# Hybrid attention and state-space trunk: the second layer's state-space preparation placed behind the first FFN's second tile, and the kernel slices stored group by group

## The chip, the cores and the metric

One core of a Trainium2 chip runs the whole program. The metric is device time in microseconds of one execution; the runs shown give a median of three.

## The reference, cut to what matters

Two layers work on 528 positions (16 learned ones and 512 inputs) of width 1024, in float32. Each layer projects the normed residual, feeds part of the result to four attention heads and part (512 channels, 32 groups of 16) to a diagonal state-space mixer, joins both with an output projection, and adds a gated FFN of width 2816.

```python
for l in range(DEPTH):
    z = _rms_norm(h, norm_mix_g[l]) @ w_in[l]
    c_q, c_kv, k_r, u = jnp.split(z, splits, axis=-1)
    attn = _mla_mixer(c_q, c_kv, k_r, ...)
    ssm = _ssm_mixer(u, ssm_a_re[l], ssm_a_im[l], ssm_log_dt[l], ...)
    mixed = jnp.concatenate([_rms_norm(attn, attn_out_g[l]), _rms_norm(ssm, ssm_out_g[l])], axis=-1)
    h = h + mixed @ w_o[l]
    hn = _rms_norm(h, norm_ffn_g[l])
    h = h + (jax.nn.silu(hn @ w_gate[l]) * (hn @ w_up[l])) @ w_down[l]
return _rms_norm(h, final_norm_g)[:, M:]
```

Inside the mixer a group's 64 complex states follow `x[t] = lam * x[t-1] + B u[t]`, and `y = Re(C x) + d * u`. `lam`, `B` and `C` come from the parameters alone, so everything made of them can be prepared before the activations are there.

## The kernel before, in words

Activations lie transposed: channels on the 128 partitions, positions along the row. Residual tiles are `h[0]` to `h[7]`. A linear layer loads weights into one of three raw buffers (`wload`, from L245), casts them on ScalarE to a rounded part `whi`, subtracts on VectorE or GpSimd to get the rest `wlo`, and multiplies both with the split activations (`product`, from L257): three terms per block of 128 x 128. In layer 0 the projections in `FULL` use plain float32 weights instead. The output products are w_oa on the attention result (`am`) and w_os on the state-space result (`sm`); their evaluation on VectorE scales the sum into `wo`, adds it to `h`, splits the new `h` into `x` for the FFN and adds its squares.

The FFN works in three phases of 7, 7 and 8 hidden tiles (`FFN_PHASES`). A tile is a gate product `ga` and an up product `ua` of 48 matmuls each; `ev_up` evaluates them on VectorE and ScalarE into `hid`. A phase ends with the products `da` back to width 1024.

The state-space part runs in chunks of 8 positions. `prep_small` (from L389) makes powers of `lam` in about 180 narrow VectorE operations, 32 groups wide; `prep_tables` (from L566) makes tables `tab` on GpSimd; `prep_mats` (from L597) makes, for each of 8 units of 4 groups, the input matrix `Xt`, the output matrix `C` and the kernel slices `K` of the 8 taps, which TensorE computes (`pk`, L643) and which go to DRAM. The last tap also holds the skip `d`. A slice of one input row is a window of the row of taps, shifted by one tap per position, with zeros behind: a transfer (L658) reads the overlapping windows from 16 partitions and writes the block of 128 x 512 that `ssm_out` (from L746) later loads as `mt` and uses as matmul weights `mt3`. Each `ya` sums a product with `mt3` on the inputs (L756) and one with `C` on the states (L757).

`prep` is a generator. Layer 0 runs it woven with its own input projection; layer 1's is advanced by `step(nxt, 2, NXT[0])` in layer 0's FFN, two pieces after every hidden tile from `NXT[1]` on, and finished by `run(nxt)`. The tile framework then sets the order of the instructions on each engine itself, from a timeline that it simulates and a priority that follows the program text; an instruction that waits for nothing can so be placed well ahead of where the text has it. Weight loads and these transfers are issued by SP, in one queue; loads of the preparation's parameters by ScalarE.

```python
            if i >= NXT[1]:
                step(nxt, 2, NXT[0])
```

The helper `after(ins)` (L203) gives a context in which the framework places instructions only behind `ins`; `latest(e)` (L199) is the instruction that engine e was given last.

Of the kernel before, what the change touches and what calls it, by code (L numbers as in the profile page):

```python
# [26 lines left out]
HC = 16  # L27
CT = 8
# [28 lines left out]
PTR = (0,0,1,0,1)  # L57
SCB = (0,1,0,0)
GLU_IN = (9,5)
NXT = (0, 0)  # L60
MB = (2,4,2,3,2)
SPL = 1
NRV = 0
# [38 lines left out]
def trunk(ctx: ExitStack, tc: tile.TileContext, A, out, dbg=None):  # L102
    nc = tc.nc
# [10 lines left out]
    V, S, P, T = nc.vector, nc.scalar, nc.gpsimd, nc.tensor  # L114
# [21 lines left out]
    def prep_tile(tag, w, bufs, name=None, dt=F32):  # L136
        return scope["prep"][1].tile([128, w], dt, tag=tag, name=name or tag, bufs=bufs)
# [61 lines left out]
    def latest(e):  # L199

        return next(i for i in reversed(nc.cur_bb.bb.instructions) if i.engine == e.engine)

    def after(ins):  # L203
        return tc.issue_after(ins) if ins is not None else nullcontext()

    def mul(e, o, a, b):
        tt(e, o, a, b, ALU.mult)
# [15 lines left out]
    h = [cp.tile([128, L], F32, name=f"h{k}") for k in range(8)]  # L223
# [160 lines left out]
    prm, mats = {}, {}  # L384
# [212 lines left out]
    def prep_mats(l, u, ea, eb):  # L597

        g0 = u * 4
        gs = slice(g0, g0 + 4)  # L600
        raw = prep_tile("bc", 448, BUFS[0])
        nc.scalar.dma_start(raw[:, 0:256], A["ssmbc"][l, u])
        b1, b2, c1, c2 = (raw[:, i * 64:(i + 1) * 64].rearrange("p (g h) -> p g h", g=4) for i in range(4))

        def bh(ap):
            return ap[:, gs].unsqueeze(2).to_broadcast([128, 4, HC])

        bb1, bb2, t = (raw[:, i * 64:(i + 1) * 64].rearrange("p (g h) -> p g h", g=4) for i in (4, 5, 6))
        for o, x, y, ci in ((bb1, b1, b2, "CIn"), (bb2, b2, b1, "CIp")):
            mul(ea, o, x, bh(prm["CR"]))  # L610
            mul(ea, t, y, bh(prm[ci]))
            tt(ea, o, o, t, ALU.add)
        yield

        def power(E, dst, tmp, x1, x2, p1, p2, n):
            def bt(ap):
                return ap.unsqueeze(2).to_broadcast([128, 4, n, HC])

            def bp(ap):
                return ap[:, :, gs].rearrange("p t g -> p g t").unsqueeze(3).to_broadcast([128, 4, n, HC])  # L620

            mul(E, dst, bt(x1), bp(p1))
            mul(E, tmp, bt(x2), bp(p2))
            tt(E, dst, dst, tmp, ALU.add)

        v4 = lambda ap: ap.rearrange("p (g t h) -> p g t h", g=4, h=HC)
        X, tmp = (prep_tile("XC", 576, BUFS[1], n)[:, 0:512] for n in ("X", "Xt"))
        power(ea if ea is eb else on('X', u), v4(X), v4(tmp), bb1, bb2, prm["prr"][:, 1:9], prm["pir"][:, 1:9], 8)
        pt = ps1.tile([128, 512], F32, tag="one", name="pt")
        for g in range(4):  # L630
            T.transpose(pt[:, g * 128:(g + 1) * 128], X[:, g * 128:(g + 1) * 128], ident)
        XT = tmp
        S.copy(XT, pt)
        nc.sync.dma_start(mats[l, u][:, 0:512], XT)
        yield
        C, tmp = (prep_tile("XC", 576, BUFS[1], n) for n in ("C", "Ct"))
        power(eb if ea is eb else on('C', u), v4(C), v4(tmp), c1, c2, prm["prs"], prm["pim"], 9)
        dst = mats["k", l, u] = dp.tile([128, 1024], F32, name=f"k{l}_{u}")
        nc.sync.dma_start(dst[:, 512:1024].rearrange("p (g w) -> p g w", g=4),
                          C.rearrange("p (g w) -> p g w", g=4)[:, :, 0:128])  # L640
        pk = ps1.tile([128, 512], F32, tag="one", name="pk")
        for g in range(4):
            T.matmul(pk[0:16, g * 128:(g + 1) * 128], bb1[:, g, :], C[:, g * 144 + 16:g * 144 + 144], start=True, stop=True)  # L643

        if u < KB:
            prm["K", u] = prep_tile(f"K{u}", 1024, 1)[0:16]
            P.memset(prm["K", u][:, 512:1024], 0.0)
        K = prm["K", u % KB]
        S.copy(K[:, 0:512].rearrange("p (t h g) -> p g t h", g=4, h=HC), pk[0:16].rearrange("p (g t h) -> p g t h", g=4, h=HC))
        skip = prep_tile("skip", 64, 2)[0:16].rearrange("p (g h) -> p g h", h=HC)  # L650
        last = K[:, 448:512].rearrange("p (h g) -> p g h", h=HC)
        mul(P, skip, ident[0:16, 0:HC].unsqueeze(1).to_broadcast([16, 4, HC]),
            skips[:, l * G + g0:l * G + g0 + 4].unsqueeze(2).to_broadcast([16, 4, HC]))
        tt(P, last, last, skip, ALU.add)
        yield
        windows = [list(d) for d in K[:, 0:512].unsqueeze(1).ap]
        windows[1] = [64, CT]
        nc.sync.dma_start(dst[:, 0:512].rearrange("(j h) w -> h j w", h=HC), bass.AP(K.tensor, K.offset, windows))  # L658
        yield

    def prep(l, ea, eb):
# [84 lines left out]
    def ssm_out(l, u, U, sv, yd):  # L746
        q, hf = divmod(u, 2)
        s = 2 if l == DEPTH - 1 else 0
        n = NC - s
        mt = ssm_tile("mt", 1024, MB[2])  # L750
        mt3, c8 = mt[:, 0:512].rearrange("p (m g) -> p g m", g=4), mt[:, 512:1024]
        nc.sync.dma_start(mt, mats["k", l, u])
        ya = ps1.tile([128, 512], F32, tag="one", name="ya")
        for i in range(4):
            o, c = slice(i * n, (i + 1) * n), slice(i * NC + s, (i + 1) * NC)
            T.matmul(ya[:, o], mt3[:, i, :], U[:, c], start=True, stop=False)  # L756
            T.matmul(ya[:, o], c8[:, i * 128:(i + 1) * 128], sv[:, c], start=False, stop=True)  # L757
        ys = ssm_tile("ys", HALF, 1)
        S.copy(ys[:, 0:4 * n], ya[:, 0:4 * n])
        nc.sync.dma_start(yd[q].rearrange("j (h g) c -> (j h) g c", h=HC)[:, hf * 4:hf * 4 + 4, :],  # L760
                          ys[:, 0:4 * n].rearrange("p (g c) -> p g c", c=n))
        yield
# [75 lines left out]
    def layer(l, nin, nout, nxt):  # L838
# [81 lines left out]
        def step(g, n=1, later=LATER[l]):  # L920
            for _ in range(n):
                tc.cur_priority += later
                next(g, None)
                tc.cur_priority -= later
# [320 lines left out]
        for ph in FFN_PHASES:  # L1245
            hid = []
            last = t0 + ph == NHT
            for i in range(t0, t0 + ph):
                wg = wload(A["w_gate"][l, i], V if i >= ONP[0] else P)
                ga = acc2("ga")  # L1250
                product(ga, wg, 0, nf.xs, nat, {PINF[1]: nf.spread} if i == 1 else {})
                if i == 0:
                    nf.F()
                wu = wload(A["w_up"][l, i], V if i >= ONP[1] else P)
                ua = acc2("ua")
                product(ua, wu, 0, nf.xs, nat, {PINF[0]: nf.summed} if i == 0 else {})
                nf.R()
                ev_up(i, ga, ua, hid)
                if i >= NXT[1]:
                    step(nxt, 2, NXT[0])  # L1260
            def down(m):
                return wload(A["w_down"][l, m][:, t0 * 128:(t0 + ph) * 128])

            def add(m, acc, c):
                hv = halves(h[m][:, c[0]:c[1]])
                tt(V, hv, pv(acc, c[1] - c[0]), hv, ALU.add)

            ends = last and l == DEPTH - 1
            for m in range(6 if ends else 8):
                w = down(m)  # L1270
                acc = acc2("da")
                product(acc, w, 0, hid, nat)
                add(m, acc, nat)
                if last:
                    nout.add(m)
                if ends and m in SCALED:
                    S.activation(h[m][:, own], h[m][:, own], AF.Copy, scale=fgain(m))
            if ends:

                ws, parts = [down(m) for m in (6, 7)], []  # L1280
                for c in ((NM, HALF + 8), (HALF + 8, L)):
                    for m in (6, 7):
                        acc = acc2("da")
                        product(acc, ws[m - 6], 0, hid, c, {TAIL[0]: parts[0].pin} if parts and m == 7 else {})
                        add(m, acc, c)
                        nout.sq.add(h[m], cols=c)
                    with after(parts[0].spread if parts and NR1 else None):
                        parts.append(Final(c, nout, "one" if parts else "norm"))
                parts[0].out(OUT[0], parts[1].then)
                parts[1].out(OUT[1])  # L1290
            t0 += ph
# [17 lines left out]
    for k in range(8):  # L1309
        if k in SQP:  # L1310
            t = single("sq")
# [110 lines left out]
```

## Time and profile before

| | |
|---|---|
| median of 3 runs | 1368.3 us (1367.06 to 1368.87) |
| profiled execution | 1364.46 us |
| its span, first to last instruction | 1362.7 us |
| mean granted TensorE clock | 0.972 |
| busy: TensorE, weight loads, VectorE | 1290.8, 1167.3, 817.0 us |
| busy: ScalarE, GpSimd | 442.0, 374.2 us |
| DMA | 145.94 MB, mean 107 GB/s |

Layer 0's input projection and attention take the first 240 us, its output products lie around 240 to 350 us, its FFN runs to about 736 us; layer 1 follows to the end. Matmul ends are modelled, so a busy share near 100% says that no wait was seen, not that the engine ran at its peak. The granted clock is the share of the full 2.4 GHz that the throttle allowed.

### The profile page before, as it was taken

The numbers are of one execution on the slowest core, as the hardware profiler recorded it, in microseconds if no ns is written. First come the engines' busy times: TensorE is split into PE (matmuls) and PEld (weight loads), VectorE is DVE, ScalarE is ACT, GpSimd is POOL, SyncE is SP. The second block draws the span as 40 slices with busy tenths as digits, with TensorE's granted clock in tenths as the row PEclk, the third lists the DMA queues.
The fourth block names the chain that finished last, engine by engine and source line by source line (L and its number), as shares of the span: only waits on it lengthen the run. The fifth ranks groups of instructions, "written<-read, shape, count | busy, mean of one in ns | idle before, by whom it ended". The sixth has DMA issues, their size and how long they took to land.

```text
span 1362.7 us, 20603 instructions
## 1 busy us (share of the span) xinstructions
PE 1290.8 (95%) x8242; PEld 1167.3 (86%) x8242; DVE 817.0 (60%) x1539; ACT 442.0 (32%) x725; POOL 374.2 (27%) x365
## 2 busy tenths in 40 slices
PE   9889999857999999999999999998999999999996
PEld 7677888847999999999999999888878888788885
DVE  8866574999654357447664468873854345435545
ACT  4212453323232123223233235661432223222231
POOL 3634233476611005205312354347200000000001
PEclk9899999978899999999999999999999999999998
DMA  5566543212433323434343535312133332232331
GB/s 190 168 169 158 149 125 90 72 47 67 133 108 101 106 90 111 105 99 120 105 109 109 186 100 177 107 47 71 54 95 95 91 105 92 82 106 93 93 94 62
DMA packets 76816, 145.94 MB, mean 107 GB/s; under 512 B 22704, under 2 KB 42672, under 8 KB 76720
## 3 DMA queue, kind: packets, MB, share of 16 engines
q1 hardware_dynamic: 73120, 141.32, 35.4%
q10 hardware_dynamic: 3600, 3.30, 0.8%
q8 instruction: 65, 1.06, 0.3%
q14 instruction: 31, 0.25, 0.1%
HBM read 121.17 MB, written 23.43 MB: 106 GB/s over the span
## 4 chain that ended last, share of the span: by engine, by line
PE 80%; DVE 11%; DMA 1%; ACT 1%; issue 1%; POOL 0%; DVEq 0%; ACTq 0%; SPq 0%; POOLq 0%
PE da L277 18%; PE ua L277 18%; PE ga L277 18%; PE acc L277 9%; PE acc L265 3%; PE ya L756 2%; PE pvo L1099 1%; PE ya L757 1%; DVE h L197 1%; PE va L721 1%; PE sc L1039 1%; DVE wo L197 1%; DVE sq L197 1%; DVE x L311 1%; PE pvo L1102 1%; PE nrb L371 1%
## 5 line engine op out<-in xcount | busy, mean ns | idle before, releaser
L253 ACT CAST whi<-raw 128x1024 fp32r<-128x1024 f32 (+3 forms) x174 | 174.2, 1001 | 567.1 <-issue 191.0
L277 PE MATMUL ga<-x,whi 128*128 128x264 f32 (+1 forms) x1056 | 227.3, 323 | 6.8 <-ACT x L310 4.8
L277 PE MATMUL ua<-x,whi 128*128 128x264 f32 (+1 forms) x1056 | 225.6, 322 | 0.0
L277 PE MATMUL da<-hid,whi 128*128 128x264 f32 (+2 forms) x1088 | 224.8, 315 | 0.0
L277 PEld LDWEIGHTS ga<-x,whi 128*128 128x128 f32 x1056 | 164.5, 190 | 24.6 <-ACT x L310 5.0
L277 PEld LDWEIGHTS da<-hid,whi 128*128 128x128 f32 x1088 | 167.1, 188 | 14.1 <-ACT whi L253 0.4
L277 PEld LDWEIGHTS ua<-x,whi 128*128 128x128 f32 x1056 | 164.9, 190 | 15.8
L197 DVE TENSOR_TENSOR wlo<-raw,whi 128x1024 fp32r<-128x1024 f32 (+1 forms) x130 | 166.7, 1282 | 13.1 <-ACT whi L253 10.7
L277 PE MATMUL da<-hid,wlo 128*128 128x264 f32 (+2 forms) x544 | 143.6, 317 | 0.2
L277 PE MATMUL ga<-x,wlo 128*128 128x264 f32 (+1 forms) x528 | 142.5, 324 | 0.7 <-POOL wlo L197 0.7
L277 PE MATMUL ua<-x,wlo 128*128 128x264 f32 (+1 forms) x528 | 142.3, 324 | 0.0
L197 POOL TENSOR_TENSOR wlo<-raw,whi 128x1024 fp32r<-128x1024 f32 (+2 forms) x44 | 95.0, 2160 | 134.3 <-ACT whi L253 115.8
L197 DVE TENSOR_TENSOR h<-da,h 128x528 f32<-128x528 f32 (+2 forms) x50 | 33.9, 677 | 133.1 <-PE da L277 132.9
L197 POOL TENSOR_TENSOR o<-h,nr 128x256 f32<-128x256 f32 x8 | 6.1, 798 | 364.8 <-ACT nr L375 364.8
L197 DVE TENSOR_TENSOR g<-ua,R 128x528 f32<-128x528 f32 (+1 forms) x44 | 30.8, 700 | 122.1 <-PE ua L277 122.0
L277 PEld LDWEIGHTS da<-hid,wlo 128*128 128x128 f32 x544 | 90.1, 188 | 8.3 <-DVE wlo L197 1.1
L277 PEld LDWEIGHTS ga<-x,wlo 128*128 128x128 f32 x528 | 88.4, 190 | 8.7 <-POOL wlo L197 1.1
L277 PEld LDWEIGHTS ua<-x,wlo 128*128 128x128 f32 x528 | 88.4, 190 | 7.4
L197 DVE TENSOR_TENSOR g<-ga,nr 128x528 f32<-128x528 f32 (+1 forms) x44 | 30.8, 699 | 90.6 <-PE ga L277 88.5
L265 PE MATMUL acc<-x,raw 128*128 128x264 f32 x320 | 78.3, 403 | 0.1
L265 PEld LDWEIGHTS acc<-x,raw 128*128 128x128 f32 x320 | 62.7, 199 | 11.7 <-ACT x L683 0.5
L277 PE MATMUL acc<-sm,whi 128*128 128x264 f32 (+1 forms) x256 | 47.2, 310 | 18.1 <-DVE wo L197 16.6
(291 smaller groups left out, 2243.7 us busy)
## 6 DMA issues: line engine op xcount, KB each, us to landing
raw<-w_gate SPq DMA_DIRECT2D x44, 512.0 KB, 3.6
raw<-w_up SPq DMA_DIRECT2D x44, 512.0 KB, 3.6
raw<-w_down SPq DMA_DIRECT2D x32, 448.0 KB, 3.4
raw<-w_in SPq DMA_DIRECT2D x20, 512.0 KB, 3.8
mat<-mat SPq DMA_DIRECT2D x16, 528.0 KB, 4.0
mt<-k SPq DMA_DIRECT2D x16, 512.0 KB, 4.6
raw<-w_down SPq DMA_DIRECT2D x16, 512.0 KB, 3.6
mat<-tab SPq DMA_DIRECT2D x16, 272.0 KB, 2.9
```

Of the source, the lines that this page charges most:

```text
L197: e.tensor_tensor(out=o, in0=a, in1=b, op=op)
L253: S.copy(hi[:, :n], raw[:, :n])
L265: T.matmul(acc[:, a, 0:hw], w[0][:, off + k * 128:off + (k + 1) * 128], xs[k][:, c0 + a * hw:c0 + (a + 1) * hw], start=k == 0, stop=k == n ...
L277: T.matmul(acc[:, a, 0:hw], wt[:, c], xs[k][:, xi, c0 + a * hw:c0 + (a + 1) * hw], start=j == 0, stop=j == len(terms) - 1)
L311: V.scalar_tensor_tensor(out=lo, in0=src, scalar=scale, in1=hi.bitcast(F32), op0=ALU.mult, op1=ALU.subtract)
L371: T.matmul(p[:, a - c0:b - c0], y[0:b - a, j:j + 1].to_broadcast([b - a, 128]), ident[0:b - a, 0:b - a], start=True, stop=True)
L721: T.matmul(va[:, i * NC:(i + 1) * NC], xt[:, i * 128:(i + 1) * 128], U[:, i * NC:(i + 1) * NC], start=True, stop=True)
L756: T.matmul(ya[:, o], mt3[:, i, :], U[:, c], start=True, stop=False)
L757: T.matmul(ya[:, o], c8[:, i * 128:(i + 1) * 128], sv[:, c], start=False, stop=True)
L1039: T.matmul(o, qn[hd][:, qs], kn[hd][:, ks], start=True, stop=False)
L1099: T.matmul(acc[:, a, 0:w], vs[hd // 2, j][0:sn, hd % 2 * 128:hd % 2 * 128 + 128], PT[j][0:sn, 0, c:c + w].bitcast(F32), start=j == 0, stop ...
L1102: T.matmul(acc[:, a, 0:w], vs[hd // 2, j][0:sn, vi, hd % 2 * 128:hd % 2 * 128 + 128], PT[j][0:sn, pi, c:c + w], start=j == 0 and z == 0, s ...
```

## The change

`NXT[1]` becomes 1: the preparation of layer 1 starts after hidden tile 1 instead of tile 0, and its first two pieces are placed only behind the last ScalarE instruction given out by then (the cast of tile 1's `hid`). It has two pieces fewer among the tiles, and so two more in `run(nxt)`. The row of taps gets one block of 256 per group, 128 taps and 128 zeros, instead of the four groups side by side within a tap; `mt3` then reads 128 neighbouring numbers per group instead of every fourth. The windows of one group are contiguous, and a store goes out as four transfers, one per group, each with runs of 512 bytes instead of 2 KB.

```diff
-NXT = (0, 0)
+NXT = (0, 1)
...
-            P.memset(prm["K", u][:, 512:1024], 0.0)
+            P.memset(prm["K", u].rearrange("p (g w) -> p g w", g=4)[:, :, 128:256], 0.0)
...
-        S.copy(K[:, 0:512].rearrange("p (t h g) -> p g t h", g=4, h=HC), pk[0:16].rearrange("p (g t h) -> p g t h", g=4, h=HC))
+        K4 = K.rearrange("p (g w) -> p g w", g=4)
+        S.copy(K4[:, :, 0:128], pk[0:16].rearrange("p (g w) -> p g w", g=4))
...
-        last = K[:, 448:512].rearrange("p (h g) -> p g h", h=HC)
+        last = K4[:, :, 112:128]
...
-        windows = [list(d) for d in K[:, 0:512].unsqueeze(1).ap]
-        windows[1] = [64, CT]
-        nc.sync.dma_start(dst[:, 0:512].rearrange("(j h) w -> h j w", h=HC), bass.AP(K.tensor, K.offset, windows))
+        for g in range(4):
+            first = K4[:, g, 0:128]
+            windows = [list(d) for d in first.unsqueeze(1).ap]
+            windows[1] = [HC, CT]
+            nc.sync.dma_start(dst[:, g * 128:(g + 1) * 128].rearrange("(j h) w -> h j w", h=HC), bass.AP(first.tensor, first.offset, windows))
...
-        mt3, c8 = mt[:, 0:512].rearrange("p (m g) -> p g m", g=4), mt[:, 512:1024]
+        mt3, c8 = mt[:, 0:512].rearrange("p (g m) -> p g m", g=4), mt[:, 512:1024]
...
                 if i >= NXT[1]:
-                    step(nxt, 2, NXT[0])
+                    with after(latest(S) if i == NXT[1] else None):
+                        step(nxt, 2, NXT[0])
```

What this does to the order of instructions is seen at three places. The first is VectorE in layer 0's second output product, before:

```order
L197 TENSOR_TENSOR h_103<-h_103,wo 128x8x66
L197 TENSOR_TENSOR e_3482<-e_3482,q 128x32
L197 TENSOR_TENSOR tq<-el,e_3452 128x32
L197 TENSOR_TENSOR e_3483<-e_3483,q 128x32
L544 COPY eh<-e_3482 128x32
L197 TENSOR_TENSOR el<-el,tq 128x32
L545 COPY eh<-e_3483 128x32
L197 TENSOR_TENSOR q<-e_3483 128x32
L197 TENSOR_TENSOR e_3496<-e_3482 128x32
L197 TENSOR_TENSOR tq<-el,e_3468 128x32
L401 SCALAR_TENSOR_TENSOR e_3497<-e_3482,e_3483 128x32
L197 TENSOR_TENSOR wo<-acc,nr 128x528
```

and with the change:

```order
L197 TENSOR_TENSOR h_103<-h_103,wo 128x8x66
L197 TENSOR_TENSOR wo<-acc,nr 128x528
L311 SCALAR_TENSOR_TENSOR x<-h_103,gains,x 128x528
L197 TENSOR_TENSOR h_104<-h_104,wo 128x8x66
L311 SCALAR_TENSOR_TENSOR x<-h_104,gains,x 128x528
L197 TENSOR_TENSOR wo<-acc,nr 128x528
L197 TENSOR_TENSOR sq<-sq 128x528
L197 TENSOR_TENSOR h_105<-h_105,wo 128x8x66
L197 TENSOR_TENSOR wo<-acc,nr 128x528
L197 TENSOR_TENSOR h_106<-h_106,wo 128x8x66
L311 SCALAR_TENSOR_TENSOR x<-h_105,gains,x 128x528
```

The operations on `e`, `el`, `eh`, `q` and `tq` (powers of `lam`, 32 wide) stand between the evaluations before, and are gone from there in the change.

The second is VectorE's list for one hidden tile late in the first FFN phase before, from one gate evaluation to the `hid`:

```order
L197 TENSOR_TENSOR g<-ga,nr 128x528
L197 TENSOR_TENSOR wlo<-raw,whi 128x1024
L1235 SCALAR_TENSOR_TENSOR g<-g 128x528
L197 TENSOR_TENSOR g<-ua,R_2894 128x528
L197 TENSOR_TENSOR g<-g 128x528
L197 TENSOR_TENSOR wlo<-raw,whi 128x1024
L197 TENSOR_TENSOR hid<-g,hid 128x528
```

and the beginning of the third tile's list in the change:

```order
L197 TENSOR_TENSOR g<-ga,nr 128x528
L401 SCALAR_TENSOR_TENSOR s<-s,r 128x32
L197 TENSOR_TENSOR wlo<-raw,whi 128x1024
L401 SCALAR_TENSOR_TENSOR s<-s,r 128x32
L1239 SCALAR_TENSOR_TENSOR g<-g 128x528
L401 SCALAR_TENSOR_TENSOR s<-s,r 128x32
L401 SCALAR_TENSOR_TENSOR dt<-s,e 128x32
L197 TENSOR_TENSOR x<-lr,dt 128x32
L406 TENSOR_SCALAR xc<-x 128x32
L397 TENSOR_SCALAR n<-xc 128x32
L398 TENSOR_SCALAR n<-n 128x32
L401 SCALAR_TENSOR_TENSOR r<-n,xc 128x32
```

Here the narrow operations (`s`, `dt`, `x`, `xc`, `n`, `r`) have come in between the evaluation and the weight splits; they go on so up to the seventh tile.

The third is SP's queue at the first units of layer 0, the rows of the old order with a minus and those of the new with a plus (the numbers name tiles):

```order
-L716 DMA mat<-mat_0_545 128x1056
-L658 DMA k_0_637<-K_644 16x8x512
-L639 DMA k_1_700<-C 128x4x128
-L592 DMA mat_2_712<-tab 128x2x272
-L592 DMA mat_3_713<-tab 128x2x272
-L752 DMA mt<-k_0_637 128x1024
+L720 DMA mat<-mat_0_545 128x1056
+L662 DMA k_0_637<-K_644 16x8x128 x4
+L639 DMA k_1_703<-C 128x4x128
+L592 DMA mat_2_718<-tab 128x2x272
+L592 DMA mat_3_719<-tab 128x2x272
+L756 DMA mt<-k_0_637 128x1024
```

The one store of the slices has become four in a row at the same place; what follows it follows still.

## Rows read from the trace of the kernel before

**Rows 1.** Busy tenths of TensorE, page part 2: 40 slices of 34 us each.

```profile
PE   9889999857999999999999999998999999999996
```

**Rows 2.** The chain that ended last, by line, page part 4.

```profile
PE da L277 18%; PE ua L277 18%; PE ga L277 18%; PE acc L277 9%; PE acc L265 3%; PE ya L756 2%; PE pvo L1099 1%; PE ya L757 1%; DVE h L197 1%; PE va L721 1%; PE sc L1039 1%; DVE wo L197 1%; DVE sq L197 1%; DVE x L311 1%; PE pvo L1102 1%; PE nrb L371 1%
```

**Rows 3.** Stretches: us, busy us (and count) of PE, PEld, DVE, ACT, POOL; PEclk, DMA share, GB/s.

```profile
140.00:240.00 100.00, 99.04 (x551) 84.51 (x549) 58.51 (x163) 48.80 (x119) 30.85 (x45) 1.00 0.43 124
240.00:352.00 112.00, 81.83 (x559) 77.81 (x559) 105.55 (x249) 32.85 (x62) 73.59 (x67) 0.84 0.23 67
352.00:465.00 113.00, 113.00 (x919) 112.24 (x918) 52.28 (x62) 31.71 (x42) 23.29 (x28) 0.99 0.38 113
780.00:917.00 137.00, 132.88 (x989) 127.16 (x988) 101.36 (x230) 70.13 (x147) 61.23 (x62) 0.98 0.38 112
```

**Rows 4.** Waits of TensorE, 240 to 352 us: total us, times, longest.

```profile
PE acc L277 <- DVE wo L197: 16.3, 4, 8.5
```

**Rows 5.** TensorE in order of time, layer 0: start, us, operation, idle before.

```profile
242.07 0.72 PE L277 MATMUL acc<-am,whi 128*128 128x264 f32 x3
...
308.06 1.25 PE L277 MATMUL acc<-sm,whi 128*128 128x264 f32 x4 [8.46 <-DVE wo L197]
```

**Rows 6.** The whole chain in order of time: start, us, what.

```profile
364.69 5.85 PE ga L277 x48
```

**Rows 7.** VectorE in order of time, layer 0's output products.

```profile
246.97 1.13 DVE L394 TENSOR_SCALAR lr<-ssmp 128x32 f32<-128x32 f32 x1 [1.10 <-DMA ssmp<-ssmp]
...
273.22 2.38 DVE L197 TENSOR_TENSOR tq<-pw 128x32 f32<-128x32 f32 x1
...
322.29 0.85 DVE L197 TENSOR_TENSOR eh<-eh,tq 128x32 f32<-128x32 f32 x1
```

**Rows 8.** GpSimd in order of time, the same place.

```profile
273.16 2.39 POOL L197 TENSOR_TENSOR wlo<-raw,whi 128x1024 fp32r<-128x1024 f32 x1 [2.28 <-ACT whi L253]
```

**Rows 9.** VectorE's groups, 246.9 to 323.2 us: busy us, mean ns.

```profile
L197 DVE TENSOR_TENSOR wo<-acc,nr 128x528 f32<-128x528 f32 x14 | 9.8, 700 | 0.0
L197 DVE TENSOR_TENSOR h<-h,wo 128x528 f32<-128x528 f32 x6 | 7.9, 1310 | 0.0
L311 DVE SCALAR_TENSOR_TENSOR x<-h,gains,x 128x528 fp32r<-128x528 f32 x5 | 4.7, 947 | 0.0
```

**Rows 10.** TensorE in order of time, layer 1's output products.

```profile
907.75 0.72 PE L277 MATMUL acc<-sm,whi 128*128 128x256 f32 x4
...
952.98 2.04 PE L371 MATMUL nrb<-cst,nw 128*128 128x128 f32 x8 [4.46 <-DVE nw L336]
```

**Rows 11.** The whole chain again, layer 1's first FFN phase.

```profile
1001.70 5.57 PE ga L277 x24
```

**Rows 12.** VectorE in order of time, the first layer's preparation.

```profile
9.47 0.19 DVE L401 SCALAR_TENSOR_TENSOR dt<-s,e 128x32 f32<-128x32 f32 x1
...
43.28 0.19 DVE L197 TENSOR_TENSOR tq<-eh,e 128x32 f32<-128x32 f32 x1
```

**Rows 13.** Groups of the whole run, weight loads of the ya products.

```profile
L756 PEld LDWEIGHTS ya<-U,mt 128*128 128x128 f32 x128 | 34.8, 319 | 0.4 <-PE acc L277 0.3
...
L757 PEld LDWEIGHTS ya<-S,mt 128*128 128x128 f32 x128 | 20.4, 198 | 0.2 <-POOL S L197 0.2
```

**Rows 14.** The chain around 151 us.

```profile
151.45 0.46 PE ya L756 x2
151.91 0.22 PE ya L757 x2
```

**Rows 15.** Instructions of tile K (ns min/median/max), and its stores' landing.

```profile
L658 SPq DMA_DIRECT2D k<-K x16: 318/325/439, 52.2 to 742.5; - x16
...
DMA to landing us min/median/max: 3.9/4.2/5.3
```

**Rows 16.** SP's issues in order of time, layer 0's start.

```profile
41.26 0.38 SPq L639 DMA_DIRECT2D k<-C  x1
41.73 0.46 SPq L634 DMA_DIRECT2D mat<-Xt  x1
```

## The prediction

> **What bounds the kernel now.** I read the page first. Its row of TensorE busy tenths falls from 9s to 8, 5 and 7 in the eighth to tenth slices, about 240 to 340 us [rows 1]; the chain that ended last is otherwise TensorE's own products [rows 2]. So outside that hole only TensorE work that disappears can shorten the run, and inside it the waits can. Then the stretches. From 240 to 352 TensorE is busy 81.83 of 112 us at a mean granted clock of 0.84 (a mix of the two levels, 2.4 and 1.2 GHz), while VectorE is busy 105.55: VectorE is the bound there. In the first FFN phase (352 to 465) TensorE is busy all 113 us and VectorE 52.28 [rows 3]. The waits of TensorE inside the hole name VectorE's `wo` first, 16.3 us, 8.5 in one piece [rows 4]. In TensorE's order of time the hole begins with the first product of w_oa at 242.07, shows that 8.46 us wait at 308.06 [rows 5], and ends when the third tile's gate product starts at 364.69 [rows 6].
>
> VectorE's own order says why. In the midst of the output products it runs the second layer's `prep_small`, from `lr` at 246.97 to the last `eh` at 322.29 [rows 7]: some 180 operations of 32 to 128 elements, no two of which fill the engine, but each of which stands ahead of a `wo` or an `h` that TensorE needs. Many are short (about 0.2 us), some are not: `tq` takes 2.38 us from 273.22, and GpSimd's `wlo` runs from 273.16 for 2.39 [rows 7, 8]. They end together, so the VectorE operation is held by the GpSimd one. Of the 76 us from `lr` to `eh`, `wo`, `h` and `x` take 9.8 + 7.9 + 4.7 [rows 9]; with the few norm and `sq` operations about 27 us are needed work, and near 49 us are preparation.
>
> **Part 1, the preparation moves behind tile 1.** It is pinned after ScalarE's last operation of the first FFN's tile 1, so no preparation operation of VectorE, GpSimd or the weight queue stands in the output products any more; VectorE's row of the change confirms it (the first order places). The stage from 242.07 to 364.69 lasts 122.6 us. Its TensorE work without waits: 16 output products of 24 matmuls and 4 FFN half tiles of 48 matmuls, at 5.85 us per 48 [rows 6]: 46.8 + 23.4, and about 6 for norm sums and spreads, 76. The waits that remain are read from layer 1, where the same code runs with no preparation beside it: first `sm` product at 907.75 [rows 10], third gate product at 1001.70 [rows 11], 93.95 us. Its own work is 16 x 12 x 5.57/24 = 44.6 [rows 11], 22.3 for four half tiles, 6.5 norm work and 5.5 attention leftovers, 79; 15 are waits. Of these 4.46 [rows 10] are a norm factor that in layer 0 has w_oa's products to hide behind; I add 2 because layer 0's `h` additions on VectorE are dearer (1.31 us mean here, in contention, against wo's 0.70 [rows 9]). So 76 + 12.5 = 88.5, a gain of **34**. Bounds: 41 if only 5 us of wait remain, 20 if GpSimd's weight splits, which stay, go on holding VectorE so that half of the waits survive.
>
> What comes back: TensorE's four groups of `pt` and `pk`, about 2.5 us, now run inside the FFN, which is TensorE bound: **+2.5**. And VectorE now does its 180 operations between tiles 2 and 6, some 50 us of TensorE time. At the start of the run the same chain went from 9.47 (`dt`) to its last operation at 43.28 [rows 12], 34 us among other work and mostly without GpSimd. In the FFN VectorE is free 60.7 of 113 us [rows 3], so five tiles of 11.7 us leave it about 31. That is a near fit, not an easy one; the weight buffers let TensorE run about half a tile ahead. What is late next, if VectorE falls behind, is `wlo`, then the next gate product; also ScalarE's cast to `whi`, because the copies of `pf` that wait for VectorE stand before it in ScalarE's order. GpSimd is nearly empty there until the first `X`; then a burst of seven large operations meets VectorE's last 25. I take **+2** for that (0 to 12).
>
> The layer's end: preparation ends one unit later in the first products of layer 1. GpSimd's `Ct` for the last unit now stands between two weight splits, a short delay against a product of 5.85 us; cover is the weight split that is one tile ahead. Nothing, or +1 if it is gone; it is in the range.
>
> **Part 2, kernel slices group by group.** Each `ya` of a group is two products. The one whose weights come from the slices (`mt3`, a step of four elements) loads its weights in 319 ns on the mean, the one with contiguous weights in 198 [rows 13], and in the chain a pair of the first takes 0.46 us, a pair of the second 0.22 [rows 14]. The change makes both contiguous: 64 pairs x 0.24 = 15.4 us of TensorE less, half in each layer. In those stretches TensorE is busy 99.04 of 100 and 132.88 of 137 us [rows 3], but work on other engines must follow its faster pace. I take 70%, **-10.5** (0.3 to 1 of it: -5 to -15).
>
> The Trainium skill, "SBUF — State Buffer", section "Door 1: The DMA port swizzle", says that memory lines are 16 bytes, that each new line costs, and that a stride is free up to "4 fp32". By that last figure a step of four fp32 would load at the contiguous rate, the change would give nothing here and the sum would be 10.5 us smaller; the 319 against 198 ns speak against that reading and for the first half of the rule.
>
> ScalarE's copy into the slices and GpSimd's `skip` addition touch the same elements as before: nothing, hidden behind other work.
>
> **Part 3, four transfers for one.** Every unit's store issues four times: 3 more issues of 0.325 us, with gaps about 1.3 us of the weight queue, x 16 units. The transfer itself lands in 4.2 us [rows 15]; nobody waits but the load of `mt`, which in most units comes much later. The six units whose store stands between loads of w_in (the third order place) delay them by 1.3 us each, with three raw buffers as cover. **+1.5** (0 to 6).
>
> The scheduler has also reordered layer 0's attention; TensorE's list has the same products there in slightly other places. I set 0, with 4 either way.
>
> **Sum:** -34 + 2.5 + 2 - 10.5 + 1.5 = -38.5. The profiled execution took 1364.46, so 1326.0; the median of the three runs shown, 1368.3, is 3.8 above it, so **1330**.
>
> **Rivals.**
> (a) The FFN pays it back. VectorE's operations behind tile 1 are held by GpSimd as often as they were in the hole (near 49 us), against 31 free: 18 us of stall instead of 2, 1346. For it: the held `tq`; against: GpSimd has no large operation until `X`. 10%.
> (b) The slices gain nothing: the longer weight load has another cause than the step, or the other engines set the pace of those stretches, or the skill's figure holds. 1340. 5%.
> (c) Half of the waits in the hole survive because GpSimd's `h` additions and weight splits hold VectorE even without preparation; layer 1 speaks against it. 1330 + 14 = 1344. 6%.
> (d) Slower. Four transfers are served one after another: if SP can issue the next only when the last has landed, a unit's store holds the queue 3 x 4.2 = 12.6 us longer. Eight units lie in layer 0's start, where loads of w_in stand behind them: 101 us of queue, of which the three raw buffers may hide a third, so 1330 + 67, about 1397. It decides from about 5 us per unit that reach the path (38.5/8). Against it: SP issues `k<-C` and `mat<-Xt` 0.47 us apart, long before the first has landed [rows 16]. 3%. The Trainium skill, "DMA: Bandwidth & Descriptors", section "Measured", says to batch transfers and calls those under 64 KB descriptor-dominated; each of the four is 64 KB, at that edge, and no run here shows the split yet.
>
> **How the numbers follow.** Forecast 76%, (a) 10, (b) 5, (c) 6, (d) 3. The range holds the forecast with its bounds and (a) to (c): from 1313 (34 becomes 41, the FFN costs nothing, the slices give all 15) to 1349 (FFN +12 and slices -5, or (a) with a slow start). A measurement of this kernel tells changes over 0.2%, 2.7 us, from none. All cases but (d) are below that, and mixtures of the bad ends reach it rarely: faster 0.95, same 0.02, slower 0.03.
>
> **What would show it.** The step is right if the third gate product starts about 34 us sooner after the first `am` product (88 us instead of 122), with VectorE's narrow operations only after tile 1 and the granted clock back near 1.0 there; if TensorE stays near 100% busy in the first FFN phase; if the weight load of `mt3` takes about 0.2 us; if the four stores issue within about 2 us. Waits of TensorE on `wlo` in tiles 3 to 6 would show (a); weight loads still near 0.32 us (b); waits on `wo` beside GpSimd's `wlo` (c); a store's four issues 4 us apart (d). A third gate product less than 15 us sooner would make the prediction wrong.

## The result, and the profile after

The changed kernel takes 1332.1 us (median of 4 runs, 1330.2 to 1332.8) against 1367.7 for the kernel before (4 runs, 1366.8 to 1368.9): ratio 0.9737, 95% interval 0.972 to 0.9754, so **35.6 us faster**, where 38.3 were predicted. The profiled execution of it took 1330.16 us, its span 1328.4. In the page's tenths the 8, 5 and 7 of [rows 1] are gone, and one 8 is left in their place (266 to 299 us). Another 8 is new, at 365 to 399 us in the FFN, and the stretch from 863 to 996 us, in layer 1, reads 8, 9, 8, 8 where the row before has one 8 in layer 1:

```profile
PE   9899999989989999999999999898899999999996
```

I cut both executions at the same four events: the first product of w_oa [rows 5], layer 0's third gate product [rows 6], the first product of layer 1, and its third gate product [rows 11]. First before, stretch by stretch, with the columns of [rows 3]:

```profile
0.00:242.07 242.07, 226.32 (x1153) 186.83 (x1153) 167.50 (x513) 90.91 (x203) 94.08 (x109) 0.97 0.53 150
242.07:364.69 122.62, 92.45 (x646) 88.76 (x645) 110.70 (x255) 35.47 (x67) 80.68 (x73) 0.85 0.25 71
364.69:736.27 371.58, 371.58 (x3048) 368.70 (x3048) 198.12 (x203) 107.94 (x135) 79.43 (x84) 1.00 0.37 107
736.27:1001.70 265.43, 252.08 (x1852) 239.28 (x1851) 168.74 (x339) 110.29 (x203) 113.86 (x91) 0.97 0.36 107
1001.70:1362.70 361.00, 348.41 (x1552) 283.76 (x1551) 171.90 (x231) 97.41 (x121) 6.14 (x8) 0.98 0.30 91
```

and the changed kernel:

```profile
0.00:239.58 239.58, 221.37 (x1152) 180.32 (x1153) 166.48 (x508) 85.19 (x201) 94.20 (x110) 0.96 0.54 152
239.58:323.04 83.46, 79.02 (x630) 77.77 (x629) 56.30 (x87) 29.02 (x43) 37.15 (x22) 0.98 0.26 80
323.04:703.14 380.10, 374.97 (x3061) 370.16 (x3060) 235.60 (x376) 112.31 (x160) 124.94 (x131) 1.00 0.38 109
703.14:967.38 264.24, 247.74 (x1854) 233.51 (x1854) 168.22 (x338) 109.25 (x203) 116.66 (x94) 0.97 0.37 109
967.38:1328.40 361.02, 348.39 (x1553) 284.03 (x1551) 171.90 (x231) 97.43 (x121) 6.13 (x8) 0.98 0.30 91
```

Row by row the change is -2.5, **-39.2**, **+8.5**, -1.2 and 0.0, together -34.3. In the second stage VectorE's busy time halves (110.70 to 56.30), TensorE's idle time falls from 30.2 to 4.4 us, and its busy time from 92.45 to 79.02 (646 products and 630), while the granted clock rises from 0.85 to 0.98; of the 16.3 us on `wo` [rows 4] 0.8 are left. In the third stage TensorE, which had not one idle microsecond before, now has 5.1, and 3.4 more of work. The fourth row is the surprise. Both layers' `ya` products got the shorter weight load that was forecast (the rows that answer to [rows 13]):

```profile
L760 PEld LDWEIGHTS ya<-U,mt 128*128 128x128 f32 x128 | 19.7, 192 | 1.9 <-PE pvv L1013 0.5 <-PE acc L277 0.5 <-ACT ys L763 0.4
L761 PEld LDWEIGHTS ya<-S,mt 128*128 128x128 f32 x128 | 19.4, 192 | 1.8 <-POOL S L197 1.8
```

and layer 1's 64 `ya<-U` products fell from 19.8 to 12.2 us of TensorE, yet its stage is only 1.2 shorter. The four stores of a unit cost little: they issue together in about 2 us and land sooner than the one did [rows 15]. First one unit's issues in SP's order of time, then the landing of all 64:

```profile
52.75 1.93 SPq L662 DMA_DIRECT2D k<-K  x4
...
DMA to landing us min/median/max: 2.0/2.7/4.7
```

Three questions follow. Does the pin alone make the hole go away, and what is the layout worth? Why did the FFN grow by 8.5? Where did layer 1's shorter weight loads go?

### The profile page after: what moved, and what is told of

Same layout as the page of the kernel before. It is cut to its first block, busy times and chain, and to the rows that moved or that the text cites. A ratio compares the mean times of both kernels' runs of the same rounds, so it can differ in the third digit from the quotient of the medians.

```text
span 1328.4 us, 20700 instructions
## 1 busy us (share of the span) xinstructions
PE 1271.5 (96%) x8242; PEld 1145.8 (86%) x8242; DVE 798.5 (60%) x1539; ACT 433.2 (33%) x725; POOL 379.1 (29%) x365
## 4 chain that ended last, share of the span: by engine, by line
PE 71%; DVE 9%; ACT 2%; issue 1%; POOL 1%; DMA 1%; DVEq 0%; SPq 0%; ACTq 0%; POOLq 0%
PE da L277 18%; PE ua L277 18%; PE ga L277 17%; PE acc L277 11%; DVE wlo L197 1%; PE acc L265 1%; PE nrb L371 1%; DVE sq L197 1%; DVE h L197 1%; PE pvo L1103 1%; PE pvo L1106 1%; PE nacc L352 1%; DVE x L311 1%; PE pk L643 1%; DVE wo L197 1%
## 5 line engine op out<-in xcount | busy, mean ns | idle before, releaser
L197 DVE TENSOR_TENSOR wlo<-raw,whi 128x1024 fp32r<-128x1024 f32 (+1 forms) x130 | 173.6, 1335 | 21.2 <-ACT whi L253 19.1
L197 POOL TENSOR_TENSOR Ct<-bc,pw 128x576 f32<-128x576 f32 x16 | 22.6, 1413 | 112.2 <-PE pk L643 112.2
```

The source lines that it names most:

```text
L197: e.tensor_tensor(out=o, in0=a, in1=b, op=op)
```

## The experiments

Twelve kernels. This table cuts each one's profiled execution at the four events above (us); ratios are those of the timed runs to the kernel before on the same chip, with the 95% interval. (In e2 and e3 the chain does not show the third gate product; there it is taken from TensorE's order of time.)

| kernel | 1: to w_oa | 2: to third gate | 3: FFN | 4: layer 1 to its third gate | 5: rest | ratio |
|---|---|---|---|---|---|---|
| before | 242.1 | 122.6 | 371.6 | 265.4 | 361.0 | 1 |
| changed | 239.6 | 83.5 | 380.1 | 264.2 | 361.0 | 0.9737 [0.972, 0.9754] |
| e1 pin alone | 244.1 | 84.5 | 380.0 | 265.0 | 361.0 | 0.978 [0.9754, 0.9806] |
| e2 layout alone | 246.9 | 120.9 | 373.1 | 264.7 | 361.2 | 0.9991 [0.9968, 1.0013] |
| e3 count alone | 242.8 | 120.1 | 374.0 | 267.9 | 361.0 | 1.0009 [0.9987, 1.003] |
| e4 four stores | 242.8 | 120.8 | 372.5 | 265.2 | 361.5 | 0.9997 [0.9985, 1.0009] |
| e5 changed again | 240.3 | 83.5 | 380.1 | 264.0 | 361.4 | 0.9714 [0.9686, 0.9742] |
| e6 GpSimd waits | 236.5 | 84.5 | 375.7 | 260.0 | 361.5 | 0.9685 [0.9638, 0.9732] |
| e7 layer 0 contiguous | 240.4 | 87.0 | 380.1 | 264.6 | 361.0 | 0.974 [0.9712, 0.9768] |
| e8 layer 1 contiguous | 244.6 | 84.9 | 380.1 | 266.1 | 361.0 | 0.9749 [0.9712, 0.9785] |
| e9 last unit on VectorE | 247.3 | 83.6 | 380.1 | 266.3 | 361.1 | 0.9785 [0.9764, 0.9806] |
| e10 e6 and e9 | 239.6 | 83.3 | 375.6 | 262.3 | 361.0 | 0.9696 [0.9671, 0.9721] |
| e11 e6 again | 238.4 | 87.0 | 375.7 | 266.3 | 361.1 | 0.9714 [0.9692, 0.9736] |
| e12 one operation on VectorE | 239.0 | 84.2 | 375.6 | 266.5 | 361.1 | 0.9717 [0.9692, 0.9743] |

### Which part carries the gain: e1 to e4

e1 is the kernel before with the two edits of the pin:

```diff
-NXT = (0, 0)
+NXT = (0, 1)
...
-                    step(nxt, 2, NXT[0])
+                    with after(latest(S) if i == NXT[1] else None):
+                        step(nxt, 2, NXT[0])
```

> Layer 1's preparation behind the second FFN tile, with the old slices and the one store. Theory (each part adds up): the stage of the output products shortens by about 34 to 39 us and the FFN of layer 0 grows by 4.5 to 8, so 1337 to 1341 us, some 5 to 10 above the changed kernel; the stretch from layer 1's first product to its third gate product stays at 265 us, and layer 0's third gate product comes near 326. Rival (the shorter weight loads of ya carry part of the hole): over 1345 us. Rival (the layout is worth nothing, since layer 1's stretch hardly moved in the changed kernel): within 2 us of the changed kernel, 1330 to 1334.

Measured: 1334.7 us against 1363.4, ratio 0.978, that is 30 us (26.5 to 33.5). Stages 2 and 3 read 84.5 and 380.0, like the changed kernel's, and stage 4 stays at 265.0. By the ratios it is 0.0043 short of the changed kernel, 5.9 us: the theory's 5 to 10.

e2 is the changed kernel with the pin's edits undone, so slices and stores alone.

> Contiguous slices and four stores, with the preparation of layer 1 where it was before. Forecast on record for this part: -10.5 + 1.5 = -9 us, so about 1359. What the trace of the changed kernel says instead (its layer 1 stretch was only 1.0 us shorter): -1 to -5 us, 1363 to 1367. Rival (slices gain nothing, stores cost 1.5): 1368 to 1370. The weight load of ya reads 0.19 us for every theory that has the layout right.

Measured: 1362.8 against 1363.4, **no change** (-4.4 to +1.8 us). Stage 5 is that of before, stage 3 1.5 us longer. Stage 1 is 4.9 us longer, and the granted clock shows where. Here are the two stretches 210 to 230 us of this kernel:

```profile
210.00:220.00 10.00, 8.89 (x34) 7.01 (x33) 2.35 (x4) 2.99 (x7) 2.66 (x2) 0.58 0.26 79
220.00:230.00 10.00, 10.00 (x28) 7.17 (x27) 3.42 (x5) 4.62 (x9) 3.97 (x3) 0.57 0.27 81
```

and of the kernel before:

```profile
210.00:220.00 10.00, 10.00 (x60) 8.53 (x60) 5.40 (x14) 5.54 (x12) 5.86 (x8) 1.00 0.51 145
220.00:230.00 10.00, 10.00 (x49) 8.45 (x48) 3.15 (x3) 3.48 (x9) 4.08 (x2) 1.00 0.27 81
```

The count of products (of mixed sizes) is the thing to see: 62 against 109 in the same 20 us. Before, TensorE had no gap there. With the shorter loads it comes to `pvo` 1.1 us before VectorE's `PT` is ready, and the granted clock reads 0.58 and 0.57: most of the stretch at the lower of the two levels. In the changed kernel's profile the same wait (1.1 us) is there and the clock stayed at 1.00.

e3 is the changed kernel with the later count, but without the pin:

```diff
-                    with after(latest(S) if i == NXT[1] else None):
-                        step(nxt, 2, NXT[0])
+                    step(nxt, 2, NXT[0])
```

> The changed kernel, its steps started one tile later (NXT 0, 1) but without the pin behind ScalarE's last instruction. Theory (the pin moves the work, the count alone doesn't, because the scheduler takes the steps out again ahead of the gate products): the same as layout alone within 3 us, 1358 to 1367, first narrow operation of layer 1 again at about 247 us. Rival (starting at the second tile is enough): 1330 to 1335.

Measured: 1363.7, ratio 1.0009. `lr` of layer 1 runs at 247.08 us, in the midst of the output products as in [rows 7]. The scheduler takes the preparation forward again; **the count alone does not move it**. The pin does, together with the later count; a pin behind tile 0 was not run.

e4 is the kernel before with its one store cut into four transfers of 128 columns, slices still interleaved:

```diff
-        nc.sync.dma_start(dst[:, 0:512]...
+        for g in range(4):
+            first = K[:, g * 128:(g + 1) * 128]
...
+            nc.sync.dma_start(dst[:, g * 128:(g + 1) * 128]...
```

> The kernel before with each unit's store cut into four transfers of 128 columns, slices still interleaved in SBUF. Forecast: 3 x 0.325 us more issues per unit, partly hidden: +1.5 us (0 to 6), 1368 to 1374. Rival (transfers serialise): 1400 or more. Rival (the four land sooner than the one, so that ya's load waits less in layer 0): 1364 to 1367.

Measured: ratio 0.9997, -2.0 to +1.2 us. The four land in 2.9 us on the median against 4.2 for the one, and their price is nothing that can be measured; serialised transfers are out.

### Why the FFN grew: e5, e6

e5 is the changed kernel unedited, run beside the next three.

> The changed kernel unedited, as the mark for the three kernels that run beside it: 1328 to 1334 us. Its first stage (to the first output product) should again end some 4 us sooner than with the old slices, unless TensorE's clock falls in it as it did in the run of the layout alone.

Measured: 1331.2 us; the stages repeat within 0.7 us, and stage 1 ended at 240.3 as expected, with the clock at 0.83 from 210 to 220.

In the changed kernel TensorE's waits of stage 3 (total us, times, longest), all between 365 and 400 us but the one on VectorE's `hid`, at 661:

```profile
PE ua L277 <- DVE wlo L197: 1.5, 1, 1.5
PE ga L277 <- DVE wlo L197: 1.4, 1, 1.4
PE da L277 <- ACT hid L307: 1.2, 1, 1.2
PE da L277 <- ACT whi L253: 0.5, 1, 0.5
PE da L277 <- DVE hid L197: 0.3, 1, 0.3
PE da L277 <- DVE wlo L197: 0.2, 1, 0.2
```

VectorE in order of time shows what makes `wlo` late:

```profile
368.17 1.27 DVE L197 TENSOR_TENSOR e<-e,q 128x32 f32<-128x32 f32 x1
369.36 2.35 DVE L197 TENSOR_TENSOR wlo<-raw,whi 128x1024 fp32r<-128x1024 f32 x1
371.63 1.39 DVE L544 COPY eh<-e 128x32 f32<-128x32 f32 x1
```

and GpSimd beside it:

```profile
368.16 1.24 POOL L197 TENSOR_TENSOR Ct<-bc,pw 128x576 f32<-128x576 f32 x1
369.35 1.28 POOL L197 TENSOR_TENSOR X<-X,Xt 128x512 f32<-128x512 f32 x1
370.59 2.40 POOL L197 TENSOR_TENSOR C<-C,Ct 128x576 f32<-128x576 f32 x1
```

An operation of 32 columns that elsewhere takes 0.18 us takes 1.27 here, and ends within 0.04 us of `Ct`; a copy of 32 columns that elsewhere takes 0.17 takes 1.39, and ends with `C`. This is the burst that the prediction named. e6 takes it away from there by data alone: VectorE writes one column of X and of C from the last value of the small preparation, so that GpSimd's first writes to them must wait (GpSimd overwrites both columns):

```diff
+        if l and not u:
+            V.tensor_copy(X[:, 0:1], prm["hi"][1][:, HIGH - 1, 0:1])
         power(ea if ea is eb else on('X', u), v4(X)...
...
+        if l and not u:
+            V.tensor_copy(C[:, 0:1], prm["hi"][1][:, HIGH - 1, 0:1])
         power(eb if ea is eb else on('C', u), v4(C)...
```

> The changed kernel with two one-element VectorE copies, by which GpSimd's first X and C of layer 1 wait for the last narrow operation of the small preparation. Theory (the FFN of layer 0 takes 8 us more than before because GpSimd's burst holds VectorE's operations, which then come late for the weight residuals): no VectorE operation of 32 columns over 0.5 us at 363 to 374, TensorE's waits at 365 to 375 (2.9 us for wlo) gone, FFN 376 to 378 instead of 380, in all 2 to 4 us less than the changed kernel. Rival (VectorE is simply full in tiles 2 to 6, whoever holds it): the same FFN within 1 us. Rival (the burst only moves onto the tables and meets the weight residuals there): the same or up to 3 us more.

Measured: the same `wlo` takes 1.21 us, GpSimd's burst begins at 371.83, and all that TensorE still waits for in stage 3 is

```profile
PE da L277 <- DVE wlo L197: 0.7, 2, 0.4
PE da L277 <- DVE hid L197: 0.3, 1, 0.3
```

Stage 3 falls from 380.1 to 375.7 us. It did so in all four kernels that had this edit (375.6 to 375.7), and in none of the others with the pin (380.0 to 380.1). VectorE does the same operations and two more, so it was not simply full: 4.4 us of the FFN's growth are VectorE held by GpSimd. The rest is work: TensorE is busy 374.68 in e6's stage, 3.1 more than before.

### Where layer 1's shorter loads went: e7 to e12

e7 and e8 make the slices contiguous in one layer only, with four stores in both (layer 0 in e7; in e8 the test is `l == 1`):

```diff
+        if l == 0:
...
+        else:
+            S.copy(K[:, 0:512].rearrange("p (t h g) -> p g t h", g=4, h=HC), ...
...
-        mt3, c8 = mt[:, 0:512].rearrange("p (g m) -> p g m", g=4), ...
+        mt3, c8 = mt[:, 0:512].rearrange("p (g m) -> p g m" if l == 0 else "p (m g) -> p g m", g=4), ...
```

> The changed kernel, but layer 1's slices interleaved as before (four stores in both layers); layer 0's stay contiguous. Theory (layer 1's 32 weight loads fewer microseconds are covered there by VectorE, ScalarE and GpSimd, which pace its attention): as the changed kernel within 2 us, layer 1's stretch 264 to 265 us although its ya product is 7 us longer on TensorE. Rival (each layer yields its half, as forecast): 3 to 5 us slower than the changed kernel, stretch of layer 1 268 us or more.

> The mirror of it: layer 1's slices contiguous, layer 0's interleaved. Theory (layer 0 yields all of it): 4 to 6 us slower than the changed kernel, the first output product near 244 instead of 240, so like the run of the pin alone. Rival (each layer its half): 3 to 5 us slower, with the first output product near 242 and layer 1's stretch below 262 us.

Measured: 1334.6 (e7) and 1337.4 us (e8) beside 1331.2. e8's stage 1 ends at 244.6, like the pin alone, so layer 0's slices shorten stage 1: it takes 242.1 to 244.6 us in the four kernels with interleaved slices there (before, e1, e4, e8) and 236.5 to 240.4 in the seven with contiguous ones whose clock did not fall to 0.6 or below from 210 to 230. Layer 1's stage is 264.6 with interleaved slices (e7) and 264.0 with contiguous ones (e5): between these two it yields next to nothing. By the medians e7 is 3.4 us slower than e5, but its profile puts that into stage 2 (87.0 against 83.5), which the edit does not touch and which e11 shows too (87.0 again); the clock withheld some 5 us there in both and some 2 in e5, and the intervals overlap.

Why, stands in layer 1's attention, 130 to 150 us behind its first product. These are the waits of the changed kernel in 830 to 850 us:

```profile
PE ya L761 <- POOL S L197: 1.7, 1, 1.7
PE pvo L1106 <- ACT PT L307: 1.0, 1, 1.0
PE ptr L1085 <- DVE PT L197: 0.7, 1, 0.7
```

The first wait is new. Before, TensorE reached the last unit's `ya<-S` at 872.35 us, and GpSimd's `S` was done at 872.30; TensorE now comes 1.7 us before it (two rows of before, one of the changed kernel):

```profile
871.61 0.69 POOL L197 TENSOR_TENSOR S<-mat,v 128x260 f32<-128x260 f32 x1
872.35 0.43 PE L757 MATMUL ya<-S,mt 128*128 128x64 f32 x2
...
835.80 0.43 PE L761 MATMUL ya<-S,mt 128*128 128x64 f32 x2 [1.71 <-POOL S L197]
```

What its clock then did:

```profile
833.00:838.00 5.00, 3.29 (x30) 3.04 (x29) 4.68 (x14) 2.88 (x9) 2.59 (x3) 1.00 0.05 16
838.00:843.00 5.00, 3.25 (x20) 2.30 (x17) 3.19 (x8) 3.90 (x12) 0.00 (x0) 0.93 0.31 79
843.00:848.00 5.00, 5.00 (x21) 4.12 (x20) 2.26 (x6) 2.85 (x7) 0.00 (x0) 0.50 0.02 5
848.00:853.00 5.00, 5.00 (x24) 4.67 (x24) 0.60 (x2) 0.47 (x2) 0.62 (x2) 0.54 0.00 0
```

TensorE was busy 3.3 of 5 us twice, and then ran ten microseconds at half clock. That is a loss of about 4.8 us, an estimate from the last two rows: 5 x 0.50 + 5 x 0.46. Cut at that `ya<-S`, the stage shows what is left: up to it the changed kernel is 3.4 us ahead, the wait included (132.7 us against 136.1), and from there it loses 2.2 (131.6 against 129.3). It loses less than 4.8 in part because before had its own low clock later on, 0.89 and 0.94 from 170 to 190 us of the stage, where the changed kernel reads 1.00. The same place in e6's execution, where TensorE had the same wait of 1.7 us:

```profile
826.60:831.60 5.00, 3.28 (x27) 3.09 (x27) 4.77 (x14) 2.82 (x8) 2.67 (x3) 0.95 0.06 21
831.60:836.60 5.00, 4.17 (x21) 2.72 (x20) 3.05 (x8) 4.04 (x12) 0.00 (x0) 0.71 0.31 79
836.60:841.60 5.00, 5.00 (x38) 4.28 (x37) 2.38 (x8) 2.98 (x7) 0.62 (x2) 1.00 0.02 5
841.60:846.60 5.00, 4.36 (x34) 3.98 (x34) 4.23 (x7) 3.59 (x8) 1.46 (x1) 1.00 0.00 0
```

Here the low clock was over sooner, and the stage took 260.0. In e11, the same kernel as e6, the three later rows read 0.50 each, and the stage took 266.3.

> The kernel with GpSimd held alone once more, for its interval and for the clock: its first run had layer 1 at full clock behind the last unit although TensorE waited there as in the changed kernel. Theory (the fall of the clock behind that wait is a matter of chance from one execution to the next): FFN 375 to 377 again, layer 1's stretch 264 us with a clock near 0.5 in it or 260 with 1.00, never 264 with 1.00. Rival (holding GpSimd itself helps layer 1): 260 again with the wait unchanged.

So the 260 was not e6's edit: the first reading holds, the wait is the same and the clock differs from one execution to the next. (e6's four timed runs, on one chip, spread too: 1319.9 us at a mean clock of 0.985, 1331.5 at 0.976.) Over all profiles: the four kernels with interleaved slices in layer 1 (before, e1, e4, e7) have no wait on `S` there, a clock of 1.00 from 130 to 160 us of the stage, and 264.6 to 265.4 us. The seven with contiguous slices and no edit to the last unit all wait 1.7 us; five fall to 0.50 to 0.53 in the ten microseconds from 140 on, e5 reads 0.87 and e6 1.00; their stage takes 260.0 to 267.9, 264.7 on the mean.

Two attempts to take the wait away failed. e9 puts all four operations of the last unit's rotation on VectorE:

```diff
-            mul(on('rot', u), gc(v)[o:o + 64]...
+            mul(V if l and u == 7 else on('rot', u), gc(v)[o:o + 64]...
...
-        mul(on('rot2', u), ct, z, ct)
+        mul(V if l and u == 7 else on('rot2', u), ct, z, ct)
...
-        tt(on('sub', u), s3[:, :, 1:NC]...
+        tt(V if l and u == 7 else on('sub', u), s3[:, :, 1:NC]...
```

> The changed kernel with the rotation of layer 1's last state-space unit (four operations: v twice, mat, S) on VectorE instead of GpSimd. Theory (in layer 1 the shorter weight loads only bring TensorE earlier to that unit's S, where it waits 1.7 us for GpSimd, after which its granted clock falls to 0.5 for some 10 us): that wait gone, granted clock 1.00 from 130 to 160 us behind layer 1's first product, stretch of layer 1 260 to 262 us instead of 264, in all 2 to 4 us less than the changed kernel (1327 to 1330). Rival (the clock falls anyway, from the waits for PT just behind, 0.7 and 1.0 us): wait on S gone, clock still 0.5 to 0.7 there, stretch 263 to 265. Rival (VectorE becomes late for the attention): stretch over 265.

> GpSimd's X and C of layer 1 held behind the small preparation, and the last unit's rotation on VectorE, together. If both theories hold the savings add up: FFN of layer 0 near 376, stretch of layer 1 near 261, 1323 to 1327 us. If the last unit does nothing: as the kernel with GpSimd held alone, 1326 to 1330.

Measured for e9: 1336.5 us where 1327 to 1330 were expected, slower than the changed kernel (0.9785 against 0.9737), and the wait grew, because VectorE ran `S` behind reductions of the attention. Its row:

```profile
PE ya L761 <- DVE S L197: 2.8, 1, 2.8
```

Its stage 1 is also the longest of all (247.3, clock 0.59 and 0.55 from 210 to 230), which this edit does not touch. e10, with GpSimd held as well, has 375.6 in stage 3 and 1323.7 us (5 runs), the lowest median, but its interval overlaps e11's (1327.3) and e6's (1328.5). It lies in the range expected for both theories, 1323 to 1327, by luck as far as the last unit goes: the wait on `S` is 2.8 us there too. e12 is e6 with only `mat` (the `rot2` line above) on VectorE.

> The kernel with GpSimd held, and of layer 1's last state-space unit one operation alone (mat, 128x264) on VectorE, S staying on GpSimd; moving all four had put S behind VectorE's attention work and made TensorE's wait longer (2.8 us). Theory (the wait on S, and the clock that falls behind it, are what takes back the shorter weight loads in layer 1): S about 1 us sooner, the wait 0.5 to 1 us instead of 1.7, granted clock behind it 0.8 or more, stretch of layer 1 260 to 263 us, 1322 to 1327 us in all. Rival (the clock falls with or without that wait): wait shorter, clock near 0.5 again, stretch 264 to 267. Rival (VectorE's extra operation delays the attention as much as S gains): stretch 264 or more at full clock.

Measured: 1325.7 us; `S` came hardly sooner (the wait is 1.5 us), the clock read 0.71 and then 0.50, stage 4 266.5. Its time lies in the theory's range, but the wait, the clock and the stage do not. With a wait so little changed this tells the theories apart no better than before. That the wait causes the fall is therefore not shown by taking it away; shown is that some fall of the clock from 130 to 160 us of the stage comes with the wait in all ten kernels that have it, and neither in the four that lack it. A longer wait did not bring a longer fall: with 2.8 us e9 reads 0.83, 0.98 and 0.85 in these three windows of ten microseconds, and e10 0.66, 0.99 and 1.00.

What the slices are worth apart from the clock can be estimated from the fourteen profiles. I cut stages 1 and 4 of each into windows of 10 us, summed what the clock withheld (a window's length times one minus its granted clock), and took the sum off the stage; it is a rough sum, since clock withheld while TensorE waits costs nothing.

| slices of that layer | stage 1: withheld | stage 1: rest | stage 4: withheld | stage 4: rest |
|---|---|---|---|---|
| interleaved (4 kernels each) | 6.8 to 10.2 | 233.9 to 235.3 | 5.1 to 6.8 | 258.4 to 259.9 |
| contiguous (10; 7 with the last unit unedited) | 5.1 to 17.1 | 228.5 to 231.8 | 5.1 to 13.7 | 254.2 to 256.2 |

The rests do not overlap, and their means lie 4.3 and 4.1 us apart. So each layer's slices do yield about 4 us, layer 1's too, and the clock took a part or all of it back in a given execution. The timed runs agree: e2's three fastest (1355.4 to 1358.8 us) have a mean clock of 0.972 to 0.974, its three slowest (1366.6 to 1371.8) 0.960 to 0.962, while all twelve runs of e4, which differs from e2 only in how the slices lie, stay within 1362.7 to 1366.8 us and 0.969 to 0.975.

## Why the prediction was right, by its steps

**The hole (taken: -34; measured: -39.2).** The mechanism was as argued, and e1 shows it alone: -38.1 in this stage. I was right that the narrow operations are the bound there; the remaining waits were too high. I read 15 us from layer 1 and took 12.5; 4.4 are left, 3.6 on ScalarE's `x` and 0.8 on `wo`. The work without waits was 79, not 76. The 15 were layer 1's stretch less its work at full clock, so lower clock counted as waiting; its idle time is 10.3 us, of which the norm factor takes 6.2 and not 4.46 (kernel before):

```profile
907.75:1001.70 93.95, 83.61 (x565) 77.10 (x564) 56.13 (x91) 30.73 (x46) 40.65 (x24) 0.95 0.22 68
...
PE nrb L371 <- DVE nw L336: 6.2, 2, 4.5
```

The other 4.1 would have come close to the 4.4 measured. Of the 39.2 us, 25.7 are idle time of TensorE and 13.4 its own work: some 3 us of it moved into the FFN, and the rest ran faster at the higher clock. The prediction had this in its sum, since it priced all work at 5.85 us per 48 products, but named no term for it.

**Work and stall in the FFN (taken: +2.5 and +2; measured: +3.4 and +5.1).** The burst of GpSimd meeting the end of VectorE's chain was the right place, and underpriced: e6 gives 4.4 us for it. The fit of VectorE's own work in five tiles held, since the FFN stalls for 1.0 us once GpSimd is out of its way. Rival (a), 18 us, is out; so is (c), since 0.8 of the 16.3 us on `wo` survive.

**The slices (taken: -10.5, bounds -5 to -15).** This term was mis-sized, and the number came near in spite of it: stages 1 and 4 got 2.5 and 1.2 us shorter, 3.7 together. The weight load fell as said (319 to 192 ns; the change of TensorE's own time in `ya` is 7.0 us in layer 0 and 7.6 in layer 1, 14.6 in all against 15.4). But "70% of it" did not reach the end: alone it gives -1.2 us (e2, -4.4 to +1.8), nearly what rival (b) said, and with the pin some 6 (0.9737 against 0.978, whose intervals just touch). Two things stood in its place. TensorE's busy 99 of 100 us [rows 3] did not mean that the others had slack at its faster pace: they were just in time, with 0.05 us between `S` and its reader, and part of the saving became waits such as those of 1.1 and 1.7 us. By the estimate above some 8.4 of the 14.6 us are left after that. And the clock, for which the term had nothing, fell behind these waits in some executions to 0.5 and took some or all of the rest. What sets off a long or a short fall is open; in stage 1 it was long in e2 and e3, and in e9 with the pin, and short or absent in the seven other kernels with contiguous slices there.

The Trainium skill, "SBUF — State Buffer", section "Door 1: The DMA port swizzle", calls a stride of up to "4 fp32" free. The weight load measured here disagrees: 319 ns at that stride, 192 contiguous, with nothing else in these instructions changed.

**The four stores (taken: +1.5, 0 to 6).** e4 puts them at -2.0 to +1.2 us: nothing. Rival (d) is out, the issues are not serialised.

**The rest.** Nothing at the layer's end and the tail (361.0 both times). The sum came out 2.7 us from the median because its errors have both signs: the hole gave 5.2 us more than taken and the stores cost 1.5 less, the FFN cost 4.0 more and the slices gave 6.8 less. That the hole carries the gain was argued and holds; that the number came so near (4.1 us in the profiled executions) is luck.

## What to carry to other kernels

Where a chain of narrow operations runs beside work that TensorE waits for, move the whole chain behind a point where the busiest engine is ahead, and check that it really stays there: here the later count did nothing without the pin. Before pricing time that is taken off a nearly full TensorE, look at how long its operands are ready before it reads them; where that is a twentieth of a microsecond, as here, the saving becomes a wait, and look at the granted clock behind that wait in more than one execution before you judge the change by one. And narrow VectorE operations that are moved beside GpSimd's large ones can be held by them (1.27 us instead of 0.18 here), so let those begin after them.

## What the runs showed of the hardware

One store of 256 KB landed in 4.2 us on the median, four of 64 KB in 2.7 to 2.9. ScalarE's copy of 16x512 elements into the slices took 1072 ns when it wrote every fourth element and 572 when it wrote in runs of 128. The same kernel's executions differ by the granted clock at a fixed place: e6 and e11, one program, took 260.0 and 266.3 us for the same stage, with 0.71, 1.00 and 1.00 against three times 0.50 in the same rows.
